# Layer 0's up projection in a two-layer decoder trunk: token sums in two passes, low parts of plain weights on GpSimd, a fifth plain feature, later writes into half-used banks

## The chip, the cores and the metric

The kernel runs on one core of a Trainium2 chip. The metric is the time of one execution on the device in microseconds (us), here the median of several executions. One of them was taken with the hardware profiler, and all readings of the trace are of that one. Engines are called TensorE (PE in the profile, its weight loads PEld), VectorE (DVE), ScalarE (ACT), GpSimd (POOL) and SyncE (SP, which issues most DMAs).

## The reference

The input is 512 tokens of 1024 channels in float32. Two layers follow one another, each a token mixer and a gated MLP, with a root-mean-square norm ahead of each and residual adds. Layer 0 mixes by causal pooling, layer 1 by sliding-window attention. The MLP is the same in both:

```python
def conv_glu_ffn(h, w_in, conv_w, conv_b, w_out):      # D_FF = 2816, CONV_W = 3
    u = h @ w_in                                       # 1024 -> 2 * 2816: values, then gates
    c = causal depthwise convolution of u over tokens, width 3, + conv_b
    a, g = c[..., :D_FF], c[..., D_FF:]
    return (a * jax.nn.silu(g)) @ w_out                # 2816 -> 1024
```

The change concerns the first half of this function in layer 0 ("up": `h @ w_in`, convolution, gate) and the order in which the second half ("down": `@ w_out`) is woven into it.

## The kernel before

**Layout and precision.** Activations lie with channels on the 128 partitions and the 512 tokens along the free axis: eight tiles `h[0..7]`. A float32 matrix product is made of three matmuls in the `fp32r` type (`mm3`, L85 to L89): both operands are split into a rounded high part and a low part, and high x high (L87), high weight x low data (L88), low weight x high data (L89) are added up in one PSUM bank. So every weight tile is fetched by DMA into `raw`, copied by ScalarE into `_h` (L101) and subtracted into `_l` (L104, on VectorE, or on GpSimd in four pieces of 256 columns where `eng` is given). Tags with a number of buffers limit how far this runs ahead: `raw` 3, `wh` and `wl` 4.

**Features.** The 2816 hidden channels are 22 "features" of 128. A feature has a gate side and a value side. A *plain* feature (the first `PLAIN` = 4) does each side as one chunk of 8 x 3 matmuls of 512 tokens into one bank. The chunks are numbered 0 to 7 in the order gate, value of feature 0, gate, value of feature 1 and so on. The norm's scale is not known when they start; so the chunks multiply the unscaled `h`, and `late` (L386) multiplies the bank by the spread scale `rb` afterwards, then convolves (`conv_sum`, L353: one ScalarE pass, L357, and two VectorE passes, L358 and L359), and applies Silu (gate) or multiplies by the gate and splits into `zh`, `zl` (value).

All later features are *half* features: value and gate sides are computed together by seven products instead of eight, each of half the tokens (256) over half of the channels, from sums of weights (R, U, W, Q, made in `half_weights`, L423) and sums of tokens `th`, `tl`. A half feature is 7 x 4 x 3 = 84 matmuls of 256 tokens. The token sums are made once by `sums` (L394): for each of four pairs of `h` tiles, six VectorE operations make seven half rows, which ScalarE copies to `th` and VectorE subtracts to `tl` (L415).

**Norm.** ScalarE squares each `h`, VectorE adds the squares into `n_acc` (L213), TensorE sums over partitions (`stats`, L219), a chain of small VectorE steps takes the inverse root (`rsqrt_mean`), and `spread` (L226) brings it back to all partitions as `rb`.

**Half features.** For each, two banks `ba` and `bx` are used by halves. Their products, in program order: R into `ba` low; the last product (W) of the feature before; W into `ba` low; R into `bx` low; U into `ba` low; U into `bx` high; Q into `ba` low. In between ScalarE copies `ba` low away three times (`s1`, `s2`, `s3`, L523, L528, L533) and VectorE changes the other halves (L530, L535, L542). The framework orders any two engines that use the same bank, also where they touch different halves.

**Down.** `down` (L448) takes the finished features in groups of `DOWN0` = 4, 5, 5, 5, 3; for each of eight output tiles it adds the group's product to `h`. Its units (three matmuls of 512) are put between the products of the half features as fills, from feature `LAG` = 6, 10, 15, 20 on; what is left comes after the last feature. The last group also makes layer 1's inputs.

**What sets the order.** A scheduler of the framework orders each engine's instructions when the program is built, by their place in the program and by its own estimate of when they become ready; those wrapped in `pin` keep their written order. At run time every engine works through its list in order. The token sums stand in the program inside chunk 3, ahead of all `late` calls. Eight PSUM banks: 0 to 5 are the ring `ps` for chunks and half features, 6 and 7 the ring `aux` for the norm and for down.

Of the kernel before, what the change touches and what calls it, by code (L numbers as in the profile page):

```python
# [37 lines left out]
DOWN0 = (4, 5, 5, 5, 3)  # L38
PLAIN = 4
# [21 lines left out]
def trunk(ctx: ExitStack, tc: tile.TileContext, x_tok, x_t, vecs, w_pool, w_kq, w_v, w_o, gain, w_in, w_half, w_down, w_end, w_tok, out):  # L61
# [133 lines left out]
    class Norm:  # L195
# [19 lines left out]
        def stats(self, ps, tiles=range(NT)):  # L215
# [5 lines left out]
            rsqrt_mean(r[:, :n], ps[:, : 2 * n].rearrange("p (a b) -> p a b", b=2)[:, :, 0], n)  # L221
# [23 lines left out]
    def pool_mixer(norm, xs, ws):  # L245
# [116 lines left out]
    def mlp_halves(fp, xs, norm, ws0, after):  # L362
# [3 lines left out]
        th, tl = [], []  # L366
# [23 lines left out]
        def spare(i, name):  # L390
            tag, bufs = (("vh", 3), ("vl", 3), ("ur", 2))[min(i // 3, 2)]
            return fp.tile([P, 1024], F32 if tag == "ur" else F32R, tag=tag, name=name, bufs=bufs)

        def sums():  # L394

            mx, px = (sm.tile([P, S], F32, tag="sq", name=f"{x}x") for x in "mp")
# [3 lines left out]
            m2, p2 = (t.rearrange("p (a b) -> p a b", a=2) for t in (mx, px))  # L400
            for p in range(4):
                th.append(fp.tile([P, 7, HS], F32R, tag="th", name=f"th{p}", bufs=4))
                tl.append(fp.tile([P, 7, HS], F32R, tag="tl", name=f"tl{p}", bufs=4))
                y, v = (spare(2 * p + i, f"ty{p}{i}").bitcast(F32).rearrange("p (a b) -> p a b", a=4) for i in range(2))
                h1, h2 = (h[c].rearrange("p (a b) -> p a b", a=2) for c in (p, p + 4))
                V.scalar_tensor_tensor(y[:, 0:4:3, :], h1, col(V_NFF + p), m2, ALU.mult, ALU.mult)
                V.scalar_tensor_tensor(y[:, 1:3, :], h2, col(V_NFF + p + 4), p2, ALU.mult, ALU.mult)
                V.tensor_tensor(v[:, 0, :], y[:, 3, :], y[:, 0, :], ALU.add)
                V.tensor_tensor(y[:, 3, :], y[:, 3, :], y[:, 2, :], ALU.add)
                V.scalar_tensor_tensor(v[:, 1, :], y[:, 2, :], -1.0, v[:, 0, :], ALU.mult, ALU.subtract)  # L410
                V.tensor_tensor(v[:, 2, :], y[:, 1, :], v[:, 1, :], ALU.subtract)
                for src, a, b in ((y, 0, 4), (v, 4, 7)):
                    x, hh, ll = (t.rearrange("p a b -> p (a b)") for t in (src[:, : b - a, :], th[p][:, a:b, :], tl[p][:, a:b, :]))
                    A.activation(hh, x, AF.Copy)
                    V.tensor_tensor(ll, x, hh.bitcast(F32), ALU.subtract)  # L415
# [60 lines left out]
        pend = [(*todo[i], pss[i]) for i in range(2)]  # L476
        ahead = load()
        ws = None
        for at in range(2, 2 * PLAIN):
            w, ps = ahead, bank("ps")  # L480
            if at + 1 < 2 * PLAIN:
                ahead = load()
            else:
# [705 lines left out]
```

## Time and profile before

| | us |
|---|---|
| median of 3 executions | 946.82 |
| lowest, highest | 946.76, 949.15 |
| the profiled execution's own time | 949.77 |
| its span, first to last instruction | 948.1 |
| TensorE busy | 903.6 |
| VectorE busy | 704.3 |
| ScalarE busy | 483.0 |
| GpSimd busy | 221.2 |

The profiled execution is 2.95 us above the median, and 1.67 us of its time lie outside the span. The plain chunks run on TensorE from 26 to 96 us of the span, the half features with the fills from then to about 390 us, the rest of down to about 425 us; attention follows to about 590 us, and layer 1's MLP to the end. A row of the page's group list reads: line, engine, operation, output tile <- input tiles (buffer numbers left out), shapes, count, busy time and mean, and the idle time of the engine just before with the instruction that ended it. In a row of waits stand the engine that waited, what it waited for, the total in us, how often, and the longest.

### The profile page before, as it was taken

To read this page: it belongs to the slowest core of one execution; us is meant where nothing else is said; L and a number is where in the kernel's file an instruction comes from. 1 tells how busy PE (TensorE), PEld (TensorE's weight loads), DVE (VectorE), ACT (ScalarE), POOL (GpSimd) and SP (SyncE) were. 2 spreads that over 40 slices of the span, in tenths; PEclk is the share of its full clock that TensorE was granted. 3 is DMA by queue.
4 is the path that set the end of the run, shared out by engine and by line. 5 is a ranking of instruction groups with operands and counts; after the bars stand their busy time and mean duration, and the time that the engine had idled before them with its cause. 6 is when DMAs were issued, how large, how long until landed. Compare 5 with 4: busy or idle time off the path is not lost.

```text
span 948.1 us, 13258 instructions
## 1 busy us (share of the span) xinstructions
PE 903.6 (95%) x4920; PEld 779.7 (82%) x4920; DVE 704.3 (74%) x1127; ACT 483.0 (51%) x782; POOL 221.2 (23%) x288
## 2 busy tenths in 40 slices
PE   8976799999989999999999999999999999999996
PEld 8755789988888978878888888888888888888885
DVE  7888688677677767576588756398896888976744
ACT  7754455555445545363588744275453444434434
POOL 3502313112131221034566513000230001210004
PEclk9986899999999999999999999999999999999999
DMA  8303654545645443243211014216458232343212
GB/s 326 112 11 90 156 175 131 164 120 144 167 122 157 109 125 106 71 136 112 90 45 46 24 45 155 71 60 217 97 118 276 95 109 69 74 147 112 96 39 89
DMA packets 37216, 109.20 MB, mean 115 GB/s; under 512 B 3872, under 2 KB 4896, under 8 KB 37152
## 3 DMA queue, kind: packets, MB, share of 16 engines
q1 hardware_dynamic: 33408, 94.74, 30.0%
q0 software_dynamic: 3744, 13.63, 8.4%
q8 instruction: 38, 0.62, 0.3%
q14 instruction: 26, 0.21, 0.1%
HBM read 106.26 MB, written 2.10 MB: 114 GB/s over the span
## 4 chain that ended last, share of the span: by engine, by line
PE 56%; DVE 2%; ACT 2%; POOL 1%; issue 1%; DMA 1%; ACTq 0%; POOLq 0%; DVEq 0%
PE bank L87 18%; PE bank L89 18%; PE bank L88 17%; PE bank L1021 1%; PE bank L1049 1%; POOL n_acc L213 1%; ACT sc L1037 1%; DMA uw_u_raw<-w_half 1%; PE bank L664 0%; DVE h L463 0%; DVE ax_l L241 0%; POOL vl L867 0%; ACT q L932 0%; PE bank L219 0%; PE bank L230 0%
## 5 line engine op out<-in xcount | busy, mean ns | idle before, releaser
L87 PE MATMUL bank<-f1x_h,wi_h 128*128 128x512 f32 x352 | 137.9, 392 | 0.0
L89 PE MATMUL bank<-f1x_h,wi_l 128*128 128x512 f32 x352 | 137.1, 389 | 0.0
L88 PE MATMUL bank<-f1x_l,wi_h 128*128 128x512 f32 x352 | 137.0, 389 | 0.0
L101 ACT ACTIVATE wi_h<-wi_raw 128x1024 fp32r<-128x1024 f32 x52 | 54.9, 1060 | 86.8 <-PE bank L88 70.0
L104 DVE TENSOR_TENSOR wi_l<-wi_raw,wi_h 128x1024 fp32r<-128x1024 f32 x48 | 58.6, 1225 | 30.5 <-ACT wi_h L101 29.7
L89 PEld LDWEIGHTS bank<-f1x_h,wi_l 128*128 128x128 f32 x352 | 66.1, 188 | 13.9
L88 PEld LDWEIGHTS bank<-f1x_l,wi_h 128*128 128x128 f32 x352 | 66.1, 188 | 13.6
L87 PEld LDWEIGHTS bank<-f1x_h,wi_h 128*128 128x128 f32 x352 | 66.1, 188 | 13.4
L437 POOL TENSOR_TENSOR uw_r_raw<-uw_r_raw,uw_u_raw 128x512 f32<-128x512 f32 x18 | 25.9, 1439 | 213.6 <-DVE uw_r_l L104 196.6
L101 ACT ACTIVATE wo_h<-wo_raw 128x640 fp32r<-128x640 f32 (+3 forms) x48 | 35.1, 734 | 46.5 <-PE bank L88 33.6
L553 DVE TENSOR_TENSOR c_u<-bank,n_rb 128x512 f32<-128x512 f32 x44 | 30.1, 688 | 22.9 <-PE bank L89 22.9
L104 DVE TENSOR_TENSOR wo_l<-wo_raw,wo_h 128x640 fp32r<-128x640 f32 (+3 forms) x44 | 35.9, 816 | 14.8 <-ACT wo_h L101 12.8
L87 PE MATMUL bank<-th,uw_v_h 128*128 128x256 f32 x144 | 41.4, 287 | 5.7 <-ACT sn L523 5.7
L87 PE MATMUL bank<-th,uw_u_h 128*128 128x256 f32 x144 | 41.5, 288 | 4.8 <-DVE bank L530 2.6
L213 POOL TENSOR_TENSOR n_acc<-n_acc,n_sq 128x512 f32<-128x512 f32 x14 | 22.5, 1604 | 89.7 <-ACT n_sq L204 89.6
L558 DVE SCALAR_TENSOR_TENSOR c_t<-c_u,vec,c_t 128x510 f32<-128x510 f32 x44 | 40.9, 933 | 1.2
L89 PE MATMUL bank<-th,uw_v_l 128*128 128x256 f32 x144 | 41.3, 287 | 0.0
L88 PE MATMUL bank<-tl,uw_v_h 128*128 128x256 f32 x144 | 41.3, 287 | 0.0
L87 PE MATMUL bank<-th,uw_r_h 128*128 128x256 f32 x144 | 40.8, 283 | 0.1
L88 PE MATMUL bank<-tl,uw_r_h 128*128 128x256 f32 x144 | 40.8, 284 | 0.0
L88 PE MATMUL bank<-tl,uw_u_h 128*128 128x256 f32 x144 | 40.7, 283 | 0.0
L89 PE MATMUL bank<-th,uw_u_l 128*128 128x256 f32 x144 | 40.7, 282 | 0.0
(434 smaller groups left out, 2833.2 us busy)
## 6 DMA issues: line engine op xcount, KB each, us to landing
wi_raw<-w_in SPq DMA_DIRECT2D x52, 512.0 KB, 3.3
uw_r_raw<-w_half SPq DMA_DIRECT2D x18, 512.0 KB, 4.4
uw_u_raw<-w_half SPq DMA_DIRECT2D x18, 512.0 KB, 3.6
uw_u_raw<-w_half POOLq DMA_DIRECT2D x18, 512.0 KB, 6.9
wo_raw<-w_down SPq DMA_DIRECT2D x24, 320.0 KB, 3.9
wt_a_raw<-w_tok SPq DMA_DIRECT2D x12, 512.0 KB, 4.5
kq_raw<-w_kq SPq DMA_DIRECT2D x10, 512.0 KB, 3.3
uw_q_raw<-w_half SPq DMA_DIRECT2D x18, 256.0 KB, 4.4
```

Source lines behind the costliest of these rows:

```text
L87: T.matmul(ps, lhsT=wh, rhs=xh, start=start, stop=False, **kw)
L88: T.matmul(ps, lhsT=wh, rhs=xl, start=False, stop=False, **kw)
L89: T.matmul(ps, lhsT=wl, rhs=xh, start=False, stop=stop, **kw)
L101: pin(A.activation(h[:, :n], raw[:, :n], AF.Copy))
L104: (eng or V).tensor_tensor(l[:, o], raw[:, o], h[:, o].bitcast(F32), ALU.subtract)
L213: eng.tensor_tensor(self.acc[:, lo:hi], self.acc[:, lo:hi], sq[:, lo:hi], ALU.add)
L437: G.tensor_tensor(r[:, :n], r[:, :n], u[:, n:], ALU.add)
L553: V.tensor_tensor(u, ps, rb, ALU.mult)
L558: V.scalar_tensor_tensor(t[:, 2:], u[:, : S - 2], cw[0], t[:, 2:], ALU.mult, ALU.add)
L1021: T.matmul(o, lhsT=qt, rhs=kt[:, kk : kk + 256], start=x == 0, stop=x == 1)
L1037: A.activation(t, t, AF.Exp, bias=neg[:, i : i + 1], scale=-1.0, accum_out=den[:, i : i + 1])
L1049: T.transpose(ps[:, i * P : (i + 1) * P], sc[i // 2][:, i % 2, kb * P : (kb + 1) * P], ident)
```

## The change

- `norm.add` for layer 0's MLP moves from the end of `pool_mixer` into `mlp_halves`; from the second tile on, the squares go to four buffers of the tag `t` instead of two of `sq`. The adds are on VectorE as before. `stats` stands in the middle of chunk 2 instead of behind it, and uses the root form (ScalarE square root, one Newton step) instead of the form with shifts and three steps; `spread` stands at the second k of chunk 3 instead of the fifth.
- `sums` is cut in two: `first_part` makes three of the seven half rows and their high and low parts for all four pairs, then `late` of chunk 0 follows, then `second_part` makes the other four half rows. The tiles for this are lent by the tags `vh` and `vl` alone, no longer by `ur`.
- The low parts of all plain chunks are made by GpSimd (`in_weights(0, ..., G)`); before, those of chunks 4 to 7 were VectorE's.
- `PLAIN` goes from 4 to 5: ten chunks. From chunk 6 on, banks 6 and 7 are put ahead in the ring `ps`; they leave it at feature 6, when down begins.
- The groups of down become 3, 5, 5, 5, 4, and the fills start at features 6, 10, 14 and 18 with the whole group spread up to the next start.
- In a half feature the VectorE subtraction of `s1` from `bx` low (L530) moves behind the feature's last product, and the addition of `s3` into `ba` high (L535) behind the Q product.

```diff
-DOWN0 = (4, 5, 5, 5, 3)
-PLAIN = 4
+DOWN0 = (3, 5, 5, 5, 4)
+PLAIN = 5
...
-        for c in range(NC):
-            norm.add(c, eng=V)
...
         def spare(i, name):
-            tag, bufs = (("vh", 3), ("vl", 3), ("ur", 2))[min(i // 3, 2)]
-            return fp.tile([P, 1024], F32 if tag == "ur" else F32R, tag=tag, name=name, bufs=bufs)
-
-        def sums():
-
+            return fp.tile([P, 1024], F32R, tag="vh" if i % 6 < 3 else "vl", name=name, bufs=3)
...
+        def split_part(src, p, a, b):
+            x, hh, ll = (t.rearrange("p a b -> p (a b)") for t in (src[:, : b - a, :], th[p][:, a:b, :], tl[p][:, a:b, :]))
+            A.activation(hh, x, AF.Copy)
+            V.tensor_tensor(ll, x, hh.bitcast(F32), ALU.subtract)
+
+        def first_part(p):
+            th.append(fp.tile([P, 7, HS], F32R, tag="th", name=f"th{p}", bufs=4))
+            tl.append(fp.tile([P, 7, HS], F32R, tag="tl", name=f"tl{p}", bufs=4))
+            y = spare(p, f"ty{p}").bitcast(F32).rearrange("p (a b) -> p a b", a=4)
+            ys.append(y)
+            m2, p2 = (blocks(t) for t in signs)
+            V.scalar_tensor_tensor(y[:, 0:4:3, :], blocks(h[p]), col(V_NFF + p), m2, ALU.mult, ALU.mult)
+            V.scalar_tensor_tensor(y[:, 1:3, :], blocks(h[p + 4]), col(V_NFF + p + 4), p2, ALU.mult, ALU.mult)
+            split_part(y, p, 0, 3)
+
+        def second_part(p):
+            y = ys[p]
+            v = spare(p + 4, f"tv{p}").bitcast(F32).rearrange("p (a b) -> p a b", a=4)
+            V.tensor_tensor(v[:, 0, :], y[:, 3, :], y[:, 2, :], ALU.add)
+            V.tensor_tensor(v[:, 1, :], y[:, 3, :], y[:, 0, :], ALU.add)
+            V.scalar_tensor_tensor(v[:, 2, :], y[:, 2, :], -1.0, v[:, 1, :], ALU.mult, ALU.subtract)
+            V.tensor_tensor(v[:, 3, :], y[:, 1, :], v[:, 2, :], ALU.subtract)
+            split_part(v, p, 3, 7)
...
+        for c in range(NC):
+            if c == 0:
+                norm.add(c)
+                continue
+            sq = norm.square(c, 0, S, fp.tile([P, S], F32, tag="t", name=f"n0_sq{c}", bufs=4))
+            V.tensor_tensor(norm.acc, norm.acc, sq, ALU.add)
...
+        def load(i):
+            if i < len(todo):
+                return ws0.pop(0) if ws0 else in_weights(0, *todo[i], G)
+
+        def chunk(i):
+            if i == 6:
+                rings["ps"][:0] = [6, 7]
+            ps = bank("ps")
+            pend.append((*todo[i], ps))
+            return ps
...
             for k in range(NC):
-                if at == 3 and k == NC // 2:
+                if at == 2 and k == NC // 2:
+                    r = norm.stats(bank("aux"), root=True)
+                if at == 3 and k == 1:
                     rb = norm.spread(bank("aux"), r)
-                    sums()
+                    signs = spread_signs()
+                    for p in range(4):
+                        first_part(p)
+                    late(*pend.pop(0))
+                    for p in range(4):
+                        second_part(p)
                 mm3(ps, part(w, k), xs[k], k == 0, k == NC - 1)
...
-        LAG = (6, 10, 15, 20)
...
-            n = NC * DOWN0[g]
-            if g == len(LAG) - 1:
-                n = 18
+        LAG = (6, 10, 14, 18, NF)
...
+            if j == LAG[0]:
+                rings["ps"] = [i for i in rings["ps"] if i < 6]
...
             product(bx[:, lo], R, 1, 1)
-            V.tensor_tensor(bx[:, lo], bx[:, lo], s1, ALU.subtract)
             fill(j, 1)
             product(ba[:, lo], U, 0, 3, False)
             A.activation(s3, ba[:, lo], AF.Copy)
             product(bx[:, hi], U, 1, 4)
-            V.tensor_tensor(ba[:, hi], bx[:, hi], s3, ALU.add)
             fill(j, 2)
             product(ba[:, lo], Q, 0, 6, False)
+            V.tensor_tensor(ba[:, hi], bx[:, hi], s3, ALU.add)
             gated(j, ba)
 
-            def last(j=j, bx=bx, W=W, s2=s2):
+            def last(j=j, bx=bx, W=W, s1=s1, s2=s2):
                 product(bx[:, hi], W, 1, 2, False)
+                V.tensor_tensor(bx[:, lo], bx[:, lo], s1, ALU.subtract)
                 V.tensor_tensor(bx[:, hi], s2, bx[:, hi], ALU.subtract)
                 valued(j, bx)
```

More of the change, by code (lines that the diff above doesn't have):

```diff
@@ L200, in __init__, with square @@
             self.acc = None
-        def square(self, c, lo, hi):
-            sq = sm.tile([P, S], F32, tag="sq", name=f"{self.name}_sq{c}_{lo}")
+        def square(self, c, lo, hi, sq=None):
+            sq = sq or sm.tile([P, S], F32, tag="sq", name=f"{self.name}_sq{c}_{lo}")
             A.activation(sq[:, lo:hi], h[c][:, lo:hi], AF.Square)
@@ L213, in add, with stats @@
             eng.tensor_tensor(self.acc[:, lo:hi], self.acc[:, lo:hi], sq[:, lo:hi], ALU.add)
-        def stats(self, ps, tiles=range(NT)):
+        def stats(self, ps, tiles=range(NT), root=False):
             n = len(tiles)
@@ L220, in stats @@
             r = small(sm, NT, 32, tag="r", name=f"{self.name}_r")
-            rsqrt_mean(r[:, :n], ps[:, : 2 * n].rearrange("p (a b) -> p a b", b=2)[:, :, 0], n)
+            rsqrt_mean(r[:, :n], ps[:, : 2 * n].rearrange("p (a b) -> p a b", b=2)[:, :, 0], n, root)
             return r
@@ L399, in sums @@
             A.activation(px, mx, AF.Copy, scale=-1.0)
[L400 to L415, printed above, removed]
@@ new lines, in spread_signs @@
+            return mx, px
+        def split_part(src, p, a, b):
[11 more added lines that the diff above has]
+            split_part(y, p, 0, 3)
@@ L467, in down @@
                 w = ahead
-        todo = [(j, s) for j in range(PLAIN) for s in (1, 0)]
-        load = lambda: ws0.pop(0) if ws0 else in_weights(0, *todo[at + 1])
-        at, r, rb, pend = 1, None, None, []
-        w, pss = [ws0.pop(0) for i in range(2)], [bank("ps") for i in range(2)]
+        for c in range(NC):
[4 more added lines that the diff above has]
+            V.tensor_tensor(norm.acc, norm.acc, sq, ALU.add)
+        todo = [(j, s) for j in range(PLAIN) for s in (1, 0)]
+        signs = rb = ws = None
+        pend, parts = [], []
+        def load(i):
[7 more added lines that the diff above has]
+            return ps
+        w, pss = [load(i) for i in range(2)], [chunk(i) for i in range(2)]
         for k in range(NC):
@@ L475, in mlp_halves @@
                 mm3(pss[i], part(w[i], k), xs[k], k == 0, k == NC - 1)
[L476 to L483, printed above, removed]
+        ahead = load(2)
+        for at in range(2, len(todo)):
+            w, ps, ahead = ahead, chunk(at), load(at + 1)
+            if at == len(todo) - 1:
                 ws = half_weights(PLAIN)
             for k in range(NC):
-                if at == 3 and k == NC // 2:
+                if at == 2 and k == NC // 2:
+                    r = norm.stats(bank("aux"), root=True)
+                if at == 3 and k == 1:
                     rb = norm.spread(bank("aux"), r)
-                    sums()
+                    signs = spread_signs()
[4 more added lines that the diff above has]
+                        second_part(p)
                 mm3(ps, part(w, k), xs[k], k == 0, k == NC - 1)
-            pend.append((*todo[at], ps))
-            if at == 2:
-                r = norm.stats(bank("aux"))
             if rb is not None:
@@ L495, in mlp_halves @@
                     late(*x)
-                pend = []
-        units, plan = [], {}
-        LAG = (6, 10, 15, 20)
-        for g, f0 in enumerate(LAG):
-            f1 = LAG[g + 1] if g + 1 < len(LAG) else NF
+                pend.clear()
+        LAG = (6, 10, 14, 18, NF)
+        plan = {}
+        for g in range(len(LAG) - 1):
+            f0, f1 = LAG[g : g + 2]
             n = NC * DOWN0[g]
-            if g == len(LAG) - 1:
-                n = 18
             for i, f in enumerate(range(f0, f1)):
```

5 lines of the change are left out of this document (4 added, 1 removed).

## The prediction, made before the changed kernel was run

> **What bounds the kernel now.** I read the page first, then busy time by stage, then TensorE's waits, and then the queue of the engine those waits named.
>
> ```profile
> PE 903.6 (95%) x4920; PEld 779.7 (82%) x4920; DVE 704.3 (74%) x1127; ACT 483.0 (51%) x782; POOL 221.2 (23%) x288
> ```
>
> TensorE is busy for 95% of the span, so only its idle stretches can be won. They lie where the change works (columns: us, busy and count of PE, PEld, DVE, ACT, POOL, granted clock, DMA share, GB/s):
>
> ```profile
> 53.30:63.60 10.30, 10.30 (x46) 8.27 (x45) 10.30 (x19) 6.98 (x9) 0.00 (x0) 1.00 0.00 0
> 63.60:70.70 7.10, 0.11 (x1) 0.00 (x1) 7.10 (x14) 3.52 (x5) 0.00 (x0) 0.71 0.00 0
> 70.70:80.30 9.60, 9.52 (x30) 7.53 (x30) 9.60 (x15) 5.46 (x7) 1.04 (x1) 0.68 0.56 144
> 80.30:88.40 8.10, 0.18 (x2) 0.00 (x0) 5.25 (x9) 3.54 (x5) 0.00 (x0) 0.70 0.12 24
> 98.30:104.10 5.80, 0.10 (x2) 0.01 (x1) 1.37 (x2) 2.06 (x4) 1.78 (x2) 0.70 0.70 203
> 125.20:420.00 294.80, 285.39 (x1862) 257.75 (x1861) 218.10 (x295) 146.10 (x226) 61.67 (x47) 1.00 0.47 131
> ```
>
> Three holes of 7.1, 8.1 and 5.8 us; after the first the clock is 0.68 for 9.6 us, which costs 9.6 x 0.32 = 3 us more. VectorE has no idle time from 53 to 80 us. TensorE's waits from 26 to 130 us, then from 125 to 440 us:
>
> ```profile
> PE bank L89 <- DVE wi_l L104: 8.0, 1, 8.0
> PE bank L87 <- ACT th L414: 7.0, 1, 7.0
> PE bank L87 <- ACT sn L523: 5.7, 1, 5.7
> PE bank L87 <- DVE bank L535: 1.5, 1, 1.5
> ```
> ```profile
> PE bank L87 <- DVE bank L535: 4.3, 4, 1.3
> PE bank L87 <- DVE bank L530: 2.6, 4, 1.1
> PE bank L87 <- ACT sn L528: 2.2, 3, 0.9
> ```
>
> The first three are one story: VectorE's queue. In 512-wide steps a chunk (one side of one plain feature, 24 matmuls) runs like this; the last two rows are 256 wide:
>
> ```profile
> 58.11 0.39 PE L87 MATMUL bank<-f0x_h,wi_h 128*128 128x512 f32 x1
> ...
> 63.32 0.39 PE L89 MATMUL bank<-f0x_h,wi_l 128*128 128x512 f32 x1
> 70.73 0.77 PE L87 MATMUL bank<-f0x_h,wi_h 128*128 128x512 f32 x1 [7.02 <-ACT th L414]
> ...
> 124.13 0.28 PE L89 MATMUL bank<-th,uw_q_l 128*128 128x256 f32 x1
> ...
> 125.20 0.28 PE L89 MATMUL bank<-th,uw_q_l 128*128 128x256 f32 x1
> ```
>
> 23 steps in 5.21 us: 0.2265 us each, 5.44 us a chunk. Nine steps in 1.07 us: 0.119 us at 256. Chunk 6 waits at 63.6 us for the bank of chunk 0, which VectorE frees only after most of the token sums (the row names ScalarE's `th`, but the first chunk's last bank read, L359, ends at 70.58 us). Chunk 7 waits for its low part, a VectorE subtraction queued behind the backlog. The third hole is ScalarE, standing in order before a transfer that was issued late:
>
> ```profile
> 102.04 1.06 ACT L419 ACTIVATE uw_u_h<-uw_u_raw 128x1024 fp32r<-128x1024 f32 x1 [5.75 <-DMA uw_u_raw<-w_half]
> ```
>
> **The change, part by part.** VectorE's prices, in the stretch 51.6 to 91 us:
>
> ```profile
> L415 DVE TENSOR_TENSOR tl<-ty,th 128x1024 fp32r<-128x1024 f32 x4 | 4.9, 1216 | 0.0
> L387 DVE TENSOR_TENSOR bank<-bank,n_rb 128x512 f32<-128x512 f32 x7 | 4.7, 690 | 2.6 <-ACT n_rb L233 2.6
> L415 DVE TENSOR_TENSOR tl<-ty,th 128x768 fp32r<-128x768 f32 x4 | 3.8, 950 | 0.0
> ...
> L406 DVE SCALAR_TENSOR_TENSOR ty<-h,vec,mx 128x512 f32<-128x512 f32 x4 | 3.0, 743 | 0.0
> L358 DVE SCALAR_TENSOR_TENSOR g_t<-bank,vec,g_t 128x511 f32<-128x511 f32 x3 | 2.2, 745 | 2.9 <-ACT g_t L357 2.9
> ...
> L374 DVE TENSOR_TENSOR a_t<-a_t,g_t 128x512 f32<-128x512 f32 x3 | 2.0, 683 | 0.0
> L410 DVE SCALAR_TENSOR_TENSOR ty<-ty,ty 128x256 f32<-128x256 f32 x4 | 1.7, 416 | 0.0
> ...
> L104 DVE TENSOR_TENSOR wi_l<-wi_raw,wi_h 128x1024 fp32r<-128x1024 f32 x1 | 1.2, 1218 | 0.0
> ```
> ```profile
> 68.51 0.74 DVE L358 SCALAR_TENSOR_TENSOR g_t<-bank,vec,g_t 128x511 f32<-128x511 f32 x1
> 69.17 0.41 DVE L409 TENSOR_TENSOR ty<-ty 128x256 f32<-128x256 f32 x1
> ```
>
> The next one starts 0.66 us after an instruction of 0.74, so each takes its mean less 0.08 us. One pair of the sums: 2 x 0.66 + 4 x 0.33 + 1.14 + 0.87 = 4.65 us, four pairs 18.6 us, in one pass or two. `late` of a gate: 0.61 + 2 x 0.66 = 1.93 us; of a value 0.6 + 0.61 more, 3.14 us.
>
> *Squares and root.* These rows set when the sums may start:
>
> ```profile
> 41.78 1.22 DVE L104 TENSOR_TENSOR wi_l<-wi_raw,wi_h 128x1024 fp32r<-128x1024 f32 x1
> 42.91 0.68 DVE L213 TENSOR_TENSOR n_acc<-n_acc,n_sq 128x512 f32<-128x512 f32 x1
> 44.74 0.16 DVE L179 TENSOR_SCALAR rs_v<-bank 128x4 f32<-128x4 f32 x1 [1.15 <-PE bank L219]
> ...
> 47.94 0.16 DVE L193 SCALAR_TENSOR_TENSOR n_r<-rs_t,rs_y 128x4 f32<-128x4 f32 x1
> 51.64 1.30 DVE L387 TENSOR_TENSOR bank<-bank,n_rb 128x512 f32<-128x512 f32 x2 [2.62 <-ACT n_rb L233]
> ```
>
> The adds stay on VectorE, but the low parts that stood between them (two of 1.14 us) go: 2.3 us. The root form replaces 3.4 us of small steps by about 1.4: 2.0 us. The spread stands three steps of k earlier (the stop at 49.9 us was 0.9 us after its inputs). So the spread scale is there at 51.6 - 5.2 = 46.4 us. The four square buffers cost nothing: ScalarE writes the squares while VectorE still adds, and idles afterwards; uncovered, a square would be 0.6 us.
>
> *Banks and bank order.* Chunks 6 and 7 write banks 6 and 7, which the norm has left; `late` of chunk 0 now stands between the passes and frees chunk 8's bank long before it is due. This takes hole one away. TensorE then ends chunk 9 at 63.55 (58.11 + 5.44) + 4 x 5.44 = 85.3 us.
>
> *Low parts on GpSimd.* They leave VectorE's backlog, so hole two goes, if GpSimd keeps up: four pieces per chunk against 5.44 us.
>
> ```profile
> L104 POOL TENSOR_TENSOR wi_l<-wi_raw,wi_h x10: 739/1182/1362, 25.2 to 36.8; 128x256 fp32r<-128x256 f32 x10
> ```
> ```profile
> L241 DVE SCALAR_TENSOR_TENSOR f0x_l<-h,vec,f0x_h x8: 746/767/1226, 25.1 to 33.9; 128x512 fp32r<-128x512 f32 x8
> ```
>
> (minimum/median/maximum, ns.) Four medians are 4.7 us: it keeps up. Behind these pieces in its queue stand the accumulating transfer and the two adds of feature 5; chunk 9's pieces end near 70 us (weight buffers are free after chunk 5 at 63.6, ScalarE 1, pieces 4.7), long before R. But the two engines stretch each other: VectorE's 0.75 us becomes 1.23, 0.48 us per piece. All ten chunks' low parts are on GpSimd; those of chunks 6 to 9, 16 pieces, fall into the sums (earlier ones are split before the scale is there): 16 x 0.48 = 7.7 us on VectorE. Bounds: 0, and 24 pieces, 11.5 us. The Trainium skill, "SBUF — State Buffer", on the engines' shared port pair, speaks against this part: it calls the pair an exclusive lock, held for the whole instruction, against VectorE work with two SBUF inputs. By that a piece would hold VectorE for its 0.74 us alone, 11.8 us in all, and the sum below would be 4.1 us less.
>
> *The backlog.* Before feature 5's first half product VectorE owes the sums (18.6), `late` of five gates and four values (9.7 + 12.6; it stands earlier in the program than the half weights) and the low part of R (1.14): 42.0 us, and 7.7. That ends at 46.4 + 49.7 = 96.1 us. TensorE, done at 85.3, waits 10.8 us: the holes become one.
>
> ```profile
> 89.49 1.22 DVE L104 TENSOR_TENSOR uw_r_l<-uw_r_raw,uw_r_h 128x1024 fp32r<-128x1024 f32 x1
> ...
> 95.81 1.22 DVE L420 TENSOR_TENSOR uw_v_l<-uw_r_raw,uw_v_h 128x1024 fp32r<-128x1024 f32 x1 [1.62 <-ACT uw_v_h L419]
> ```
>
> From R's low part to W's, through GpSimd's two adds and ScalarE, took 6.3 us (90.7 to 97.0): W is ready at 102.4. R's two products fill 24 x 0.119 + 3 (slow clock) = 5.9 us of it. U's buffers are no longer lent to the sums, so its transfers start early and hole three stays away; if they came as late as now, 5.7 us return. Then W, U, U, Q and the next R, 60 x 0.119 = 7.1 us: 109.5 us. Before, the same point (feature 5's Q and feature 6's R done) is 125.3. **Plain stage: -15.8 us**, the fifth plain feature's dearer matmuls (48 x 0.2265 against 84 x 0.119, +0.9 us) included. Bounds: VectorE off the path, TensorE alone gives 85.3 + 84 x 0.119 = 95.3, -30; with 11.5 us of contention, ScalarE idles like now (2.9) and U late again, -6.
>
> *Later writes.* From 125 us TensorE no longer waits for L535 and L530 (4.3 + 2.6): Q and U now need only ScalarE's copies, which have a product or a fill behind them. Some of it comes back as waits like L528's; I take **-5 us**, bounds -6.9 and 0.
>
> *Fills and tail.* The fills only change places, as many matmuls as before; 46 units of `down` after the last feature become 32, all of the last group, whose fourth input is the last feature's value. From its last product to that value: two 0.34, Identity 0.7, two 0.66, 0.6, copy 0.6, 0.61 = 4.5 us, against three units (2.0 us), or six with both banks (4.1). I take **+1.5 us** (0.4 to 2.5), less the 1.3 us waited there now.
>
> Sum: -15.8 - 5 + 1.5 - 1.3 = -20.6. Against the profiled execution's own 949.77 us (span 948.1) that is 929.2; that execution was 2.95 us over the median of 946.82, so the forecast is 926.2 us.
>
> **The rivals.** *A, VectorE is not the wait:* R's low part is ordered ahead of waiting `late`s, or GpSimd hardly disturbs. For: ScalarE idles and the scheduler moves ready work up. Against: chunk 7's low part stood behind the same backlog. Plain stage -25, together -30: 917.
>
> *B, a full lock:* every one of the 24 pieces holds VectorE for 0.74 us, 17.8 instead of 7.7: 10.1 us later, 936.3. For: GpSimd's pieces went from 0.74 to 1.18 as well. Against: VectorE's 0.75 us grew by 0.48, not 0.74. The Trainium skill's page named above states this lock.
>
> *C, the holes only move:* VectorE's same work decides and R is not ready until 114 to 118 us, 18 to 22 us past my sum: 944 to 948, no change. Against: the queue sum for before (51.6 to 90.7) closes with what it idled.
>
> *D, slower:* `s1` now stays until `last`, in a ring of five `sn` tiles, so the next feature's `s3` needs VectorE's subtraction first, and Q behind it. Between them lie some 5 to 8 us of products; if VectorE ran later than that, TensorE would wait in each of 17 features. It decides from 1.2 us each (20.6 / 17); at 2 us each 34 us come back: 960. Against: VectorE is busy 74% there (218 of 295 us).
>
> **How the numbers follow.** Forecast 0.5, A 0.2, B 0.2, C 0.06, D 0.04. A measurement of this kernel can tell about 0.3%, 2.8 us. Faster is forecast, A, B and the rest of C (0.02): 0.92; same 0.04; slower 0.04. The forecast's own range is 920 to 933; A's and B's bounds widen it to 913 to 939, which leaves out C, D and the outer end of A.
>
> **What would show it.** Right: no TensorE hole before chunk 9; one hole of about 11 us before the first 256-wide product, ended by `uw_r_l`; GpSimd pieces near 1.2 us and VectorE's sums stretched beside them; no L530 or L535 row among TensorE's waits; a short wait near the end of `down`. Wrong: a hole at `wi_l` on GpSimd, `uw_r_l` before 90 or after 103 us, or waits on `sn` in most features.

## The result, and the profile after

| | before | after |
|---|---|---|
| median of 12 executions, us | 949.38 | 944.22 |
| lowest to highest | 946.76 to 951.57 | 941.54 to 945.83 |
| profiled execution, own time (span) | 949.77 (948.1) | 942.96 (941.3) |

The ratio is 0.9946, with a 95% interval of 0.9932 to 0.996: the change gains about 5 us. The forecast was 926.2 us, with a range of 913 to 939, so the sign was right and the size a quarter of what was forecast. (The three executions of before shown above are among these twelve; counted from their median of 946.82 us, the forecast's ratio was 0.978.)

Measured in the two profiled executions (-6.8 us), the landmarks of the prediction divide it so. The point (feature 5's Q and feature 6's R done) moved from 125.3 to 122.3 us: -3.0, where -15.8 was forecast. From there to attention's first matmul it took 294.5 us after 298.8: -4.35, where -5 + 1.5 - 1.3 = -4.8 was forecast. The rest of the program is +0.5. So in number the second part came as forecast and the first did not; whether the second part's terms were right is tested below. The rows for it, from TensorE's timeline of after (start and duration in us; the rows of before are those at 125.20 above and the last one here, which is of before):

```profile
122.20 0.28 PE L89 MATMUL bank<-th,uw_q_l 128*128 128x256 f32 x1
...
416.78 0.39 PE L87 MATMUL bank<-ax_h,kq_h 128*128 128x512 f32 x1
```
```profile
424.13 0.74 PE L87 MATMUL bank<-ax_h,kq_h 128*128 128x512 f32 x2
```

TensorE's waits in after, from 26 to 130 us and then from 125 to 440 us:

```profile
PE bank L89 <- DVE uw_r_l L104: 6.0, 1, 6.0
PE bank L87 <- issue: 4.0, 1, 4.0
PE bank L87 <- DVE g_t L356: 2.9, 1, 2.9
PE bank L87 <- ACT sn L554: 2.4, 1, 2.4
PE bank L87 <- ACT sn L549: 2.2, 1, 2.2
PE bank L219 <- DVE n_acc L481: 2.2, 1, 2.2
```
```profile
PE bank L87 <- ACT sn L549: 3.0, 2, 1.9
PE bank L87 <- ACT wo_h L101: 2.6, 2, 2.0
PE bank L87 <- DVE h L470: 1.1, 2, 0.8
```

The three holes of before are gone: nothing of size stops TensorE before the end of chunk 9 but 2.2 us for the norm's sum. The waits on the two later writes are gone as well. In their place stands one broken hole from 86.6 to 103.5 us (waits of 4.0, 2.9, 1.0 and 6.0 us), which ends with `uw_r_l`, R's low part, as forecast, but 7.35 us later than forecast. The busy time by stage of after (columns as in the prediction: us, busy and count of PE, PEld, DVE, ACT, POOL, granted clock, DMA share, GB/s) shows why:

```profile
70.00:78.00 8.00, 8.00 (x37) 6.63 (x36) 7.97 (x13) 3.08 (x4) 7.92 (x4) 1.00 0.01 2
78.00:87.70 9.70, 8.58 (x38) 6.76 (x36) 0.03 (x1) 1.64 (x3) 1.04 (x2) 1.00 0.49 108
87.70:103.50 15.80, 2.92 (x8) 2.00 (x8) 15.80 (x25) 9.97 (x15) 0.00 (x0) 0.57 0.00 1
103.50:125.20 21.70, 17.14 (x102) 16.65 (x103) 14.96 (x18) 8.75 (x14) 8.68 (x7) 0.76 0.59 154
```

From 78.0 to 87.7 us VectorE, whose queue sets the end of the hole, stands still. The timelines of ScalarE, VectorE and GpSimd there name the chain (in brackets the idle time before an instruction, and what ended it):

```profile
86.06 1.06 ACT L426 ACTIVATE uw_u_h<-uw_u_raw 128x1024 fp32r<-128x1024 f32 x1 [10.78 <-DMA uw_u_raw<-w_half]
87.03 0.61 ACT L379 ACTIVATE z0h<-a_t 128x512 fp32r<-128x512 f32 x1
```
```profile
87.67 0.69 DVE L380 TENSOR_TENSOR z0l<-a_t,z0h 128x512 fp32r<-128x512 f32 x1 [9.70 <-ACT z0h L379]
```
```profile
70.08 7.98 POOL L104 TENSOR_TENSOR wi_l<-wi_raw,wi_h 128x256 fp32r<-128x256 f32 x4 [3.74 <-ACT wi_h L101]
78.01 1.02 POOL L441 DMA_DIRECT2D uw_u_raw<-w_half  x1
...
105.27 2.13 POOL L445 TENSOR_TENSOR uw_r_raw<-uw_r_raw 128x512 f32<-128x512 f32 x1
107.35 0.89 POOL L441 DMA_DIRECT2D uw_u_raw<-w_half  x1
```

U is fetched by two transfers: a plain one by SyncE and an accumulating one (L441) on GpSimd's queue. SyncE's were issued at 29 us, so the buffers were free early, as the prediction said. The accumulating one stands, by its place in the program, behind chunk 9's low part, which is GpSimd's own new work, and goes out at 78.0. It lands 8 us later. ScalarE waits for it in order (10.8 us) with `z0h` behind it; VectorE waits 9.7 us for `z0h`. For feature 6 the same comes again: its accumulating transfer goes out at 107.35 behind the two adds for W, ScalarE waits 5.2 us and TensorE 2.4 us (the row of L554).

### The profile page after: what moved, and what is told of

It is laid out like the page before. It is cut to its first block, busy times and chain, and to the rows that moved or that the text cites. A ratio compares the mean times of both kernels' runs of the same rounds, so it can differ in the third digit from the quotient of the medians.

```text
span 941.3 us, 13168 instructions
## 1 busy us (share of the span) xinstructions
PE 902.2 (96%) x4884; PEld 780.2 (83%) x4884; DVE 696.5 (74%) x1110; ACT 483.9 (51%) x778; POOL 242.8 (26%) x309
## 4 chain that ended last, share of the span: by engine, by line
PE 82%; DVE 7%; ACT 4%; DMA 3%; issue 2%; POOL 2%; DVEq 0%; ACTq 0%; POOLq 0%
PE bank L87 26%; PE bank L88 26%; PE bank L89 26%; DMA uw_u_raw<-w_half 2%; DMA uw_r_raw<-w_half 1%; PE bank L1047 1%; PE bank L1075 1%; POOL wi_l L104 1%; DVE n_acc L481 1%; PE bank L285 1%; PE bank L252 1%; ACT sc L1063 1%; ACT h L329 0%; DVE g_t L355 0%; DVE g_t L356 0%
## 5 line engine op out<-in xcount | busy, mean ns | idle before, releaser
L101 ACT ACTIVATE wi_h<-wi_raw 128x1024 fp32r<-128x1024 f32 x54 | 57.0, 1060 | 86.4 <-PE bank L88 71.3
L444 POOL TENSOR_TENSOR uw_r_raw<-uw_r_raw,uw_u_raw 128x512 f32<-128x512 f32 x17 | 23.0, 1354 | 215.1 <-DVE uw_r_l L104 208.6
L88 PEld LDWEIGHTS bank<-f1x_l,wi_h 128*128 128x128 f32 x352 | 66.1, 188 | 13.4
L104 DVE TENSOR_TENSOR wi_l<-wi_raw,wi_h 128x1024 fp32r<-128x1024 f32 x44 | 53.8, 1225 | 29.4 <-ACT wi_h L101 28.6
L104 POOL TENSOR_TENSOR wi_l<-wi_raw,wi_h 128x256 fp32r<-128x256 f32 x40 | 41.0, 1057 | 30.4 <-ACT wi_h L101 18.7
L89 PE MATMUL bank<-th,uw_r_l 128*128 128x256 f32 x136 | 39.5, 292 | 6.0 <-DVE uw_r_l L104 6.0
L87 PE MATMUL bank<-th,uw_v_h 128*128 128x256 f32 x136 | 39.0, 287 | 5.2 <-ACT sn L549 5.2
L87 PE MATMUL bank<-th,uw_u_h 128*128 128x256 f32 x136 | 39.2, 288 | 2.4 <-ACT sn L554 2.4
L427 DVE TENSOR_TENSOR uw_v_l<-uw_r_raw,uw_v_h 128x1024 fp32r<-128x1024 f32 x17 | 20.8, 1225 | 25.6 <-ACT uw_v_h L426 25.4
```

The source lines that it names most:

```text
L87: T.matmul(ps, lhsT=wh, rhs=xh, start=start, stop=False, **kw)
L88: T.matmul(ps, lhsT=wh, rhs=xl, start=False, stop=False, **kw)
L89: T.matmul(ps, lhsT=wl, rhs=xh, start=False, stop=stop, **kw)
L101: pin(A.activation(h[:, :n], raw[:, :n], AF.Copy))
L104: (eng or V).tensor_tensor(l[:, o], raw[:, o], h[:, o].bitcast(F32), ALU.subtract)
L427: V.tensor_tensor(y, raw, x.bitcast(F32), ALU.subtract)
```

## The experiments

Times are medians; a ratio is against runs of the kernel before on the same chip. Theory 1 at first: U's accumulating transfer, held in GpSimd's queue, keeps some 10 us of the gain. The rival: VectorE and GpSimd disturb each other more than the sum allowed.

### U's transfers written earlier

`u5_early` writes the two transfers of U for feature 5 ahead of chunk 7's weights; `u_ahead` besides this writes each later feature's one feature earlier.

```diff
+        raw_u = {}
+
+        def fetch_u(j):
+            u = raw_u[j] = fp.tile([P, 1024], F32, tag="ur", name=f"uw{j}_u_raw", bufs=2)
+            u2 = u.rearrange("p (a b) -> p a b", a=2)
+            nc.sync.dma_start(u2, w_half[j - PLAIN][:, 0:4:2, :])
+            pin(G.dma_start(u2, w_half[j - PLAIN][:, 2:4, :], accum_op=ALU.add))
...
             nc.sync.dma_start(q[:, :n], src[:, 3, :])
-            pin(G.dma_start(u2, src[:, 2:4, :], accum_op=ALU.add))
+            if j + 1 < NF:          # u_ahead only
+                fetch_u(j + 1)
...
+            if at == 6:
+                fetch_u(PLAIN)
             w, ps, ahead = ahead, chunk(at), load(at + 1)
```

> The changed kernel, with the two transfers of feature 5's U weights written ahead of chunk 7's low part instead of behind chunk 9's. Every VectorE and ScalarE instruction keeps its place; only GpSimd's queue has one transfer earlier. Theory 1 (queue): in the changed kernel this accumulating transfer leaves at 78.0 us, behind chunk 9's low part, lands at 86.1, and ScalarE's in-order wait for it (10.8 us) idles VectorE for 9.7 us; with it early that idle time goes, R's low part ends near 94 us instead of 103.5, and the kernel takes about 935 us. Rival 2 (contention): GpSimd's low parts stretch VectorE's sums and that sets the end; the time stays within 2 us of the changed kernel's 944.

> As u5_early, and each later feature's U transfers stand one feature earlier in GpSimd's queue (ahead of the adds of the feature before). Theory 1: ScalarE's second wait for U (5.2 us, at 114.5 us in the changed kernel) goes too, with TensorE's 2.4 us hole behind it and some of the slow clock after it: 3 to 5 us less than u5_early, near 931 us. Rival 2: as u5_early, within 2 us of 944.

Measured: `u5_early` 935.40 us, ratio 0.987 (0.985 to 0.9891); `u_ahead` 927.69, ratio 0.9783 (0.9766 to 0.98). Against after that is 8.8 and 16.5 us faster (7 and 15.5 by the ratios), where the rival expected 2 or less. ScalarE and VectorE in `u_ahead`:

```profile
73.15 1.04 ACT L426 ACTIVATE uw_u_h<-uw_u_raw 128x1024 fp32r<-128x1024 f32 x1
...
78.17 0.63 ACT L379 ACTIVATE z0h<-a_t 128x512 fp32r<-128x512 f32 x1 [2.08 <-DVE a_t L371]
```
```profile
93.73 1.22 DVE L104 TENSOR_TENSOR uw_r_l<-uw_r_raw,uw_r_h 128x1024 fp32r<-128x1024 f32 x1
```

ScalarE no longer waits for U, VectorE does not stop, and R's low part ends at 94.95 us (forecast 96.1; in after 103.45). With U in time the time is 1.5 us from the forecast, in part by luck (see below). `u_ahead` gained 7.7 us over `u5_early`, where its Theory 1 had 3 to 5; in the two profiled executions (spans of 931.7 and 927.1 us) it is 4.6.

### The low parts back on VectorE

`low9_dve` gives the low part of chunk 9 back to VectorE, `low_dve` those of chunks 4 to 9; U's transfers stay where after has them in the program.

```diff
-                return ws0.pop(0) if ws0 else in_weights(0, *todo[i], G)
+                return ws0.pop(0) if ws0 else in_weights(0, *todo[i], G if i < 9 else None)   # low9_dve
+                return ws0.pop(0) if ws0 else in_weights(0, *todo[i])                         # low_dve
```

> The changed kernel with chunk 9's low part on VectorE and all others on GpSimd. Theory 1: the accumulating transfer follows chunk 8's pieces at 66.3 us and lands near 74, before ScalarE comes to it at 75.3; VectorE's idle 9.7 us go and 1.1 us of work are added: about 936 us. Rival 2: only chunk 9's four pieces leave the sums, at most 2 us: 942 to 945.

> The changed kernel with the low parts of chunks 4 to 9 on VectorE, as before the change. Theory 1: the transfer is early and the idle 9.7 us go, the stretching (about 4 us) too, but six low parts of 1.14 us return to VectorE's queue and the last of them stand behind the backlog, so TensorE waits for them again: 938 to 946 us, not better than low9_dve. Rival 2: the sums run unstretched and this is the fastest of the four, under 936 us.

Measured: `low9_dve` 934.15 us, ratio 0.9848 (0.983 to 0.9866); `low_dve` 939.35, ratio 0.9906 (0.9891 to 0.9921). In `low9_dve` the transfer goes out 11.6 us earlier, right behind chunk 8's pieces, and VectorE does not stop for it (its longest stop between 52 and 105 us is 0.4 us):

```profile
66.44 1.04 POOL L441 DMA_DIRECT2D uw_u_raw<-w_half  x1
```

Taking GpSimd's work off in full is the slower of the two, against the rival, which wanted it fastest. In both kernels TensorE now waits for a low part that VectorE makes behind its backlog, as in hole two of before (TensorE's waits up to 130 us, `low9_dve` and then `low_dve`):

```profile
PE bank L89 <- DVE wi_l L104: 10.0, 1, 10.0
PE bank L87 <- ACT sn L549: 3.3, 1, 3.3
```
```profile
PE bank L89 <- DVE wi_l L104: 10.9, 1, 10.9
PE bank L87 <- ACT sn L549: 4.2, 1, 4.2
```

In `low9_dve` this hole (82.5 to 92.5 us, ahead of chunk 9's low products) takes the place of the wait for R's low part, which ends at 94.8 us and costs no wait of its own. In `low_dve` the hole stands in chunk 7 and ends at 84.75 us; the low parts of chunks 8 and 9 still follow, and chunk 9 ends 2.7 us later than in `low9_dve`.

So the queue is the cause: `u5_early` and `low9_dve` get the transfer out early in two different ways, with nearly all the rest of the change as it was, and both take away VectorE's stop. The price of moving the low parts to GpSimd was the transfer behind them. `low_dve`, which undoes most of that move, is even 4.9 us faster than after; with U early in the program the move pays (927.69 against 939.35).

### What the contention cost

`ahead_no_lows` is `u_ahead` without the 16 pieces of chunks 6 to 9.

```diff
             if i < len(todo):
+                if i >= 6:
+                    raw = fetch(w_in[0][todo[i]], D, f"wi0_{i}")
+                    x = wp.tile([P, 1024], F32R, tag="wh", name=f"wi0_{i}_h")
+                    A.activation(x, raw, AF.Copy)
+                    return x, lows[5]
-                return ws0.pop(0) if ws0 else in_weights(0, *todo[i], G)
+                x = ws0.pop(0) if ws0 else in_weights(0, *todo[i], G)
+                lows[i] = x[1]
+                return x
```

> This is u_ahead without GpSimd's low parts of chunks 6 to 9: the 16 pieces are left out, and these chunks multiply by the low part of chunk 5 in their place (so the output is not the reference's); all matmuls stay. It takes away what the forecast priced at 16 x 0.48 = 7.7 us on VectorE, and nothing else of VectorE's. In u_ahead VectorE was busy without a gap from 50.0 to 94.95 us for work counted as 42.0 us, so Theory 1 (the contention cost it 2.9 us): R's low part ends 2.5 to 3.5 us earlier, at 91.5 to 92.5, and the time falls by 3 to 4 us, to about 924. Rival (the forecast's 7.7 us, the work itself being shorter than counted): R's low part ends near 87, TensorE hardly waits for it, and the time falls by 6 to 8 us, to about 920.

Measured: 922.41 us, ratio 0.9715 (0.9688 to 0.9741), against 927.69 and 0.9771 of `u_ahead` beside it. VectorE's queue from the scale to R's low part, first and last row in `ahead_no_lows`:

```profile
49.30 1.30 DVE L384 TENSOR_TENSOR bank<-bank,n_rb 128x512 f32<-128x512 f32 x2 [1.27 <-ACT n_rb L233]
...
88.11 1.22 DVE L104 TENSOR_TENSOR uw_r_l<-uw_r_raw,uw_r_h 128x1024 fp32r<-128x1024 f32 x1
```

49.30 to 89.33 is 40.0 us of work without GpSimd beside it; in `u_ahead` it was 44.9 (50.0 to 94.95), with VectorE busy without a gap and the same 66 rows in both. So the contention cost 4.9 us, 0.31 per piece, between the 2.9 of Theory 1 and the 7.7 of the forecast, and the bare work was 40.0 instead of the 42.0 counted. Both theories missed the size.

### The later writes and the groups of down

`ahead_early_writes` is `u_ahead` with the subtraction of `s1` and the addition of `s3` at their old places; `ahead_old_groups` is `u_ahead` with down's old groups; `ahead_both_old` has both; `before_later` is the kernel before with the later writes alone; `u_ahead_again` repeats `u_ahead` beside `ahead_both_old`.

```diff
             product(bx[:, lo], R, 1, 1)
+            V.tensor_tensor(bx[:, lo], bx[:, lo], s1, ALU.subtract)      # early writes
...
             product(bx[:, hi], U, 1, 4)
+            V.tensor_tensor(ba[:, hi], bx[:, hi], s3, ALU.add)           # early writes
...
-DOWN0 = (3, 5, 5, 5, 4)
-        LAG = (6, 10, 14, 18, NF)
+DOWN0 = (4, 5, 5, 5, 3)                                                  # old groups
+        LAG = (6, 10, 15, 20, NF)                                        # old groups
...
```

> This is u_ahead (927.69 us) with the two later writes undone: the subtraction of s1 and the addition of s3 stand again where the kernel before had them. Theory 1 (the forecast's term of -5 us for the later writes is real and independent of the plain stage): 5 us slower than u_ahead, 932.7 us (930.5 to 934.6, the term's bounds 0 and 6.9 less the ends), and the waits on bank from the subtraction and the addition come back among TensorE's waits with 5 to 7 us in all. Rival (those waits only passed on to the next one, so that taking them away was worth nothing): within 1 us of u_ahead, with the same waits shown.

> The kernel before with nothing but the two later writes. Theory 1: the term of -5 us alone, a ratio of 0.9947 (0.9935 to 0.9965), with no bank wait from the addition or the subtraction in the half features. Rival (the late subtraction holds the tile s1 back, and TensorE then waits for ScalarE's copies instead, the mechanism of rival D of the prediction): ratio 0.998 or more, and waits on sn grow by what the bank waits lost.

> This is u_ahead with down's groups and fills of the kernel before (4, 5, 5, 5, 3 features; from features 6, 10, 15, 20). The forecast has +1.5 - 1.3 us for the new groups: Theory 1: within 1 us of u_ahead, 927.7 us, with the short wait near the end of down smaller or gone. Rival (the old groups leave more features without fills, so TensorE waits for ScalarE and VectorE there, and the new groups were worth more than the forecast said): 3 us or more slower than u_ahead, with waits on sn or bank between 200 and 390 us.

> The same as u_ahead, so that the three others have it beside them on one chip. Both theories: a ratio within 0.002 of the 0.9783 measured first, some 928 us.

> This is u_ahead with both the later writes undone and down's old groups and fill places. Each of the two undone alone moved u_ahead by less than 2 us. Theory 1 (the two edits take away the same waits: a TensorE that has fills behind nearly every product does not notice that VectorE's write into the other half comes early, and with the late writes the missing fills do not matter): undoing both costs 3 to 6 us against u_ahead, about what the forecast booked for the later writes alone, with 5 to 7 us of waits on bank from the subtraction and the addition back between 125 and 440 us. Rival (the two add up, each worth what it was alone): within 2 us of u_ahead, with hardly any such waits.

| kernel | us | ratio (95%) |
|---|---|---|
| `before_later` | 946.54 | 0.9971 (0.9954 to 0.9988) |
| `ahead_early_writes` | 930.56 | 0.9801 (0.9784 to 0.9819) |
| `ahead_old_groups` | 927.43 | 0.9766 (0.9752 to 0.9781) |
| `u_ahead_again` | 927.69 | 0.9771 (0.9746 to 0.9797) |
| `ahead_both_old` | 929.76 | 0.9798 (0.9771 to 0.9826) |

The groups were worth nothing either way, as forecast (+1.5 - 1.3). The later writes are worth about half their term: 2.75 us in the kernel before (1.1 to 4.4 by the interval). In `u_ahead` undoing them cost 1.7 us by the ratio to the first measurement of `u_ahead` and 2.9 by the medians; there the intervals overlap, the two profiled spans (927.1 and 927.2) show no difference, and of the old waits 0.4 us came back where 5 to 7 were expected. Undoing writes and groups together cost 2.1 us and not 3 to 6, with overlapping intervals as well. So the two terms account for the -4.35 us from the point to attention's first matmul only at the outer end of that first interval; what else is in it was not followed. Where part of the term went can be seen in `before_later`, TensorE's waits from 125 to 440 us:

```profile
PE bank L87 <- ACT wo_h L101: 4.5, 3, 1.9
PE bank L87 <- DVE bank L536: 2.2, 1, 2.2
```

In before these were 4.3 (L535) and 2.6 (L530) and none on `wo_h`. One wait of 2.2 us is still for a later write (L536 is the moved addition of `s3`); the others went, and three times TensorE came to wait for ScalarE's copy of down's weights instead. In `ahead_both_old` only 1.6 us of the old waits come back:

```profile
PE bank L87 <- ACT sn L561: 2.0, 2, 1.3
PE bank L87 <- DVE bank L568: 1.6, 2, 0.8
```

### R's low part ahead of the late steps

In `u_ahead` TensorE still waits 6.3 us for R's low part. `ahead_r_first` moves the `late` calls of chunks 2 to 9 behind it; `r_first_stats` then puts the norm's sum and the spread three steps of k later.

```diff
-            if rb is not None:
-                for x in pend:
-                    late(*x)
-                pend.clear()
+            if at in (3, len(todo) - 1):
+                for i in range(1 if at == 3 else 2):
+                    late(*pend.pop(0))
...
                 ws = half_weights(j + 1)
+            for i in range(min(2, len(pend))):
+                late(*pend.pop(0))
...
+            if j == PLAIN:
+                for i in range(2):
+                    late(*pend.pop(0))
             fill(j, 3)
```

```diff
-                if at == 2 and k == NC // 2:
+                if at == 2 and k == NC - 1:
-                if at == 3 and k == 1:
+                if at == 3 and k == NC // 2:
```

> This is u_ahead with the late steps of the plain chunks 2 to 9 written behind the half weights of feature 5 (chunks 2 and 3), of feature 6 (4 and 5) and inside features 5 and 6 (6 to 9), so that VectorE makes the low parts of R, U, W and Q of feature 5 ahead of them. In u_ahead TensorE, done with the plain chunks at 86 us, waits 6.3 us for R's low part and 5.0 us on sn, and works at a reduced clock after. Theory 1 (VectorE's queue up to R's low part is what is left): these waits and the slow clock go, 7 to 10 us faster than u_ahead, 918 to 921 us. Rival (VectorE's total work up to the middle of the half features decides; the backlog only moves and TensorE waits for bank or sn in features 5 to 9 instead): within 3 us of u_ahead, 925 to 930 us.

> This is ahead_r_first (921.87 us) with the norm's partition sum three steps of k later in chunk 2, and the spread three steps later in chunk 3. TensorE stood 2.2 us in front of that sum, waiting for the last square to be added. Theory 1: the wait goes, the scale is ready at the same time because the squares set it, and the time falls by about 2 us, to 920. Rival (the wait only decided when TensorE starts chunk 3, and the scale now comes 2 us later to VectorE, which is the bound up to feature 6): within 1 us of ahead_r_first.

Measured: `ahead_r_first` 921.87 us, ratio 0.971 (0.9695 to 0.9726), 22.3 us faster than after and the fastest kernel of the study. That is 5.8 us faster than `u_ahead`, a little short of Theory 1's 7 to 10 and twice the rival's 3. Its stages, against the same of `u_ahead` in the second fence:

```profile
86.40:96.00 9.60, 3.56 (x21) 2.79 (x20) 9.60 (x14) 5.62 (x10) 3.75 (x3) 0.88 0.78 189
96.00:110.00 14.00, 13.71 (x98) 13.50 (x97) 11.81 (x17) 8.03 (x13) 3.84 (x3) 0.84 0.38 87
```
```profile
86.40:96.00 9.60, 2.59 (x14) 2.14 (x13) 9.60 (x15) 4.60 (x7) 0.82 (x1) 0.79 0.00 1
96.00:110.00 14.00, 11.30 (x71) 10.81 (x70) 11.57 (x13) 6.61 (x10) 7.13 (x5) 0.78 0.61 163
```

The mean granted clock is higher (0.88 and 0.84 against 0.79 and 0.78), and TensorE's work after 96 us is denser. VectorE's backlog was moved to where TensorE has products to do.

`r_first_stats` was to save 2 us more. It took 930.01, ratio 0.9799 (0.9772 to 0.9826): 8 us slower, against both its theories. The wait for the sum fell from 2.2 to 0.7 us, but a new one of 8.2 stands at 85 us. GpSimd's pieces (minimum, median and maximum in ns, first and last start) and its queue, in that kernel:

```profile
L104 POOL TENSOR_TENSOR wi_l<-wi_raw,wi_h x7: 737/1030/7997, 61.8 to 80.8; 128x256 fp32r<-128x256 f32 x7
```
```profile
61.81 20.46 POOL L104 TENSOR_TENSOR wi_l<-wi_raw,wi_h 128x256 fp32r<-128x256 f32 x8 [2.46 <-ACT wi_h L101]
82.22 0.86 POOL L436 DMA_DIRECT2D uw_u_raw<-w_half  x1
...
84.49 1.29 POOL L455 TENSOR_TENSOR uw_r_raw<-uw_r_raw 128x512 f32<-128x512 f32 x1
```

Eight pieces take 20.5 us here, and 10.6 in `ahead_r_first` (3.38 and 7.26 for four each): single pieces are stretched to 8.00 us. W's adds stand behind them, and ScalarE waits 8.5 us for the second add with the steps of `late` behind it. TensorE starts feature 5 at 93.77 us, 0.2 us after VectorE's last read of a chunk's bank (L356, done at 93.56); the profile names no releaser, so that it waited for this bank is inferred. The edit itself touches no piece: it shifts the scale by 0.8 us against `u_ahead` (50.85 after 50.03), and with it which VectorE instructions run beside which piece. That this alone stretched the pieces is the reading of the two traces; no further run tests it.

## Why the prediction was wrong, point by point

**The step that failed** is the sentence "U's buffers are no longer lent to the sums, so its transfers start early and hole three stays away". The buffers and SyncE's transfers behaved so. GpSimd's accumulating transfer did not: the prediction itself put it behind chunk 9's pieces in GpSimd's queue, and asked only whether these would be done before R (it had them done near 70 us; they were done at 78: ScalarE, with the copies of the token sums ahead in its order, made chunk 9's high part only from 68.96 us, and the four pieces took 7.98 us instead of 4.7). Even at 70 us the transfer, which took 8 us to land, would have come near 78, behind 75.3, where ScalarE was free for it; that is an estimate from these rows. It did not follow the second way out of that transfer, ScalarE's in-order copy of U and `z0h` behind it, on which VectorE's backlog hangs. The price was given too ("if they came as late as now, 5.7 us return"), but as TensorE's wait of before; the stall fell on VectorE, ahead of R, and then again for feature 6. `u5_early` changes this step for feature 5 alone and takes back 8.8 us; `u_ahead` does it for every feature and takes back 16.5.

| step | forecast | measured |
|---|---|---|
| scale ready | 46.4 us | 49.8 (after), 50.0 (`u_ahead`) |
| chunk 9 done | 85.3 | 86.6 |
| VectorE's work to R's low part, without GpSimd | 42.0 | 40.0 (`ahead_no_lows`) |
| GpSimd's pieces on it | 7.7 | 4.9 (`u_ahead` less `ahead_no_lows`) |
| VectorE's stop for U | 0 | 9.7 (after), 0 (`u_ahead`) |
| R's low part done | 96.1 | 103.45 (after), 94.95 (`u_ahead`) |
| from R's low part to W's | 6.3 | 6.3 in both |
| from R's low part to the point | 13.4 | 18.9 (after), 16.2 (`u_ahead`) |
| later writes | -5 | -2.75 (`before_later`), -1.7 to -2.9, not clear of noise (`u_ahead`) |
| new groups, tail | +0.2 | 0 (`ahead_old_groups`) |

**The start of the sums.** The forecast had 5.2 us gained on the scale; it was 1.8. The row of after:

```profile
49.80 1.30 DVE L384 TENSOR_TENSOR bank<-bank,n_rb 128x512 f32<-128x512 f32 x2 [1.21 <-ACT n_rb L233]
```

The last square is added at 42.84 us in after and at 43.59 in before, 0.75 us earlier, where 2.3 were forecast; the root saved 1.1 us instead of 2.0, and the earlier spread nothing instead of 0.9. VectorE's work here now runs beside GpSimd's pieces: seven adds took 7.0 us, two small steps of the root 0.66 us each instead of 0.16 (L192, L193), the four of `n_d` 2.34 instead of 0.88. The prediction took the low parts out of VectorE's queue there, and did not charge their contention at this place.

**Contention.** Rivals A and B were answered by `ahead_no_lows`: neither none nor 17.8 us, but 4.9; and in the trace of after R's low part stands behind the waiting `late` steps, as the forecast had it and A did not. In `u_ahead` the start came 3.6 us late, the contention was 2.8 us less than forecast, and the work 2.0 us shorter than counted. That R's low part was forecast within 1.2 us of `u_ahead` is the luck of these three errors.

**After R.** The slow clock was booked only under R's products, where W's arrival hides it. In `u_ahead` the granted clock is still 0.83 from W's arrival to the point:

```profile
101.10:111.20 10.10, 9.93 (x67) 9.64 (x67) 9.03 (x11) 5.45 (x10) 4.30 (x3) 0.83 0.79 206
```

9.93 us of work at that clock lose 9.93 x 0.17 = 1.7 us, an estimate, of the 2.8 beyond the forecast; the rest was not followed. In after the clock is 0.57 and then 0.76 up to 125 us, and the wait for U of feature 6 comes on top.

**Luck in the near hit of `u_ahead`.** Its parts are -14.2 us up to the point, -7.9 from there to attention's first matmul and +1.0 for the rest of the program (spans), against -15.8, -4.8 and 0. The later writes are in the -7.9 with about half of their 5 us, and the earlier transfers of the later features, which the forecast had not counted as a gain, with part of the 3.5 us by which this stretch is shorter than in after.

**A bound that does not add up.** The outer bound of the plain stage was given as -6. From its own terms (3.8 us more contention, 2.9 of ScalarE, 5.7 of U) it is -15.8 + 12.4 = -3.4; measured was -3.0.

By its own test the prediction fell: `uw_r_l` after 103 us was named as what would show it wrong.

**What held.** Holes one and two went, one hole ended by `uw_r_l` took their place, GpSimd kept up with TensorE (though its pieces were not near 1.2 us: the eight of chunks 8 and 9 have a median of 0.92 and a maximum of 2.77), and rival D did not come: with `s1` held longer, waits on `sn` after 125 us are 3.0 us in all. Rival C gave the right time (944 to 948) by luck, for another reason: it had VectorE too busy, and the trace has it idle for 9.7 us.

## What to carry to other kernels

When work is moved to an engine, read its queue on past that work: what is issued from there, transfers too, is now as late as the new work, and each consumer of it has to be followed, together with what stands behind that consumer in its own order. A low price for one wait is not the price of the step; the first engine to stop may be another than the one that stopped before. And waits at one place, here the early writes and the copies of down's weights, can stand in for each other: the 6.9 us that the list gave to the two writes were more than twice what removing them gained.

## What the runs showed of the hardware

**GpSimd can be held for many of its own durations.** A 128x256 subtraction of 0.74 us took up to 2.77 us in after and 8.00 us in `r_first_stats`, while VectorE ran back to back and at its normal pace. VectorE's timeline at the end of the 8.00 us piece (64.2 to 72.2 us), and at the end of the next slow one (73.2 to 80.2):

```profile
71.18 0.41 DVE L420 SCALAR_TENSOR_TENSOR tv<-ty,tv 128x256 f32<-128x256 f32 x1
71.51 0.73 DVE L355 SCALAR_TENSOR_TENSOR a_t<-bank,vec,a_t 128x511 f32<-128x511 f32 x1
...
77.77 1.21 DVE L427 TENSOR_TENSOR uw_u_l<-uw_u_raw,uw_u_h 128x1024 fp32r<-128x1024 f32 x1
78.91 0.67 DVE L104 TENSOR_TENSOR uw_q_l<-uw_q_raw,uw_q_h 128x512 fp32r<-128x512 f32 x1
```

The first piece ends while VectorE reads a PSUM bank (L355, from 71.51), the second 0.6 us after VectorE runs out of work (78.91 + 0.67), about the time of one undisturbed piece. In between VectorE's instructions have both inputs in SBUF. Three long pieces of after end like the first, at 72.8, 75.0 and 77.3 us, each while VectorE reads a bank (L355 from 72.17, L356 from 74.30, L384 from 76.69). The Trainium skill, "SBUF — State Buffer", "Who interferes with whom", says that a VectorE instruction with two SBUF inputs contends with a GpSimd instruction that reads SBUF, and "SBUF: two separate sides" that whoever starts first holds the shared pair for its whole instruction, the other being blocked. The trace agrees with the blocking (8.00 us), and with the PSUM reader letting GpSimd in. But over a run of instructions the side that holds the pair can keep it, in this trace VectorE for 7 us; where the two took turns, in the rows of before that the prediction read, it was 0.48 us a piece. Which of the two comes about was not settled here.

**The clock follows the stretch before.** Over the hole of after the granted clock was 0.57, and 0.76 over the next 21.7 us, in which TensorE was busy for 17.1. This is no slow rise. TensorE's 256-wide products stand 0.12 or 0.21 us apart in that timeline, and the spacing changes at 110.3, 113.7, 117.1 and 120.5 us, 3.4 us apart each time. Cut at these places and one and two such steps ahead (columns as above):

```profile
103.49:106.90 3.41, 3.14 (x13) 2.85 (x13) 3.41 (x4) 0.00 (x0) 3.14 (x2) 0.50 0.00 0
106.90:110.30 3.40, 1.49 (x12) 1.49 (x13) 1.81 (x4) 1.85 (x3) 1.33 (x2) 1.00 0.70 178
110.30:113.70 3.40, 3.40 (x18) 3.40 (x18) 1.78 (x3) 0.00 (x0) 0.00 (x0) 0.51 0.91 200
113.70:117.10 3.40, 1.01 (x8) 0.81 (x7) 0.84 (x2) 2.52 (x4) 2.31 (x2) 0.99 0.41 161
117.10:120.50 3.40, 3.40 (x19) 3.40 (x18) 3.40 (x5) 1.63 (x3) 1.03 (x2) 0.51 0.49 64
120.50:123.90 3.40, 3.40 (x30) 3.40 (x30) 2.76 (x4) 2.28 (x4) 0.00 (x0) 0.99 1.01 299
```

A stretch has the full clock where TensorE was busy for 3.1 to 3.4 us of the stretch before, and half of it where it was busy for 1.5 or 1.0. The waits inside those two were only 2.2 and 2.4 us long, and each was followed by 3.4 us at half clock, in which 1.7 us of work are lost by that figure (an estimate). This is read from one trace; no run was made to test it.
